# A seven-product MLP: four products of a pair accumulate in one PSUM bank that is read between them, two in a second bank

## The chip, the core and the metric

The kernel runs on one core of a Trainium2 chip. The metric is the device time of one execution in microseconds. Before the change the median of three runs is 2589.54 us (2586.69 to 2592.21).

The engines are called as the profile calls them: PE is TensorE's matrix multiplication and PEld its loading of weights, DVE is VectorE, ACT is ScalarE, POOL is GpSimd, and SP issues most of the DMAs. PSUM is the small memory into which matmuls write; a bank of it holds one result of 128 x 512 numbers here. ACT and DVE can read it. The kernel's tile framework puts in all the semaphores: an instruction that reads or writes a tile waits for the earlier ones on that tile. Each engine has one queue, whose order is fixed when the program is built.

## The reference

One decoder layer over 2048 tokens of width 1024 in f32: a mixer (retention and pooling heads), a cross-attention into 256 memory tokens, a gated MLP, each behind a row norm and with a residual, and a final norm. The change touches the MLP alone (`w_up` is 1024 x 5632, `w_down` 2816 x 1024):

```
def conv_glu_ffn(h, w_up, conv_w, conv_b, w_down):
    a = h @ w_up
    a1, a2 = a shifted by one and by two tokens
    c = conv_w[0] * a2 + conv_w[1] * a1 + conv_w[2] * a + conv_b
    gate, val = jnp.split(c, 2, axis=-1)
    return (jax.nn.silu(gate) * val) @ w_down
```

## The kernel before

**Passes.** Every f32 product is made of three matmuls on a high and a low half of each operand (`passes`, lines L226, L227 and L228: high by high, high by low, low by high). The high half is a rounded copy, the low half what the rounding left.

**Seven products.** Both halves of the MLP multiply in blocks of two by two with seven products in place of eight, in the manner of Strassen and Winograd. The weights' blocks are a11, a12, a21, a22 (rows: the two output tiles of a pair; columns: two halves of the contraction), and the right-hand side's are the two halves of the contraction by two halves of 512 tokens. Such a set of seven is a `Member`: `Up` (a gate column tile and its value column tile, 22 for each half of the tokens, 44 in all) or `Down` (two output tiles of 128 features and a third of the contraction: 4 pairs, 3 thirds, 2 halves of the tokens, 24 in all). A product is 4 x 3 matmuls of 128 x 128 by 128 x 512; in the first third of Down it is 3 x 3.

**The order.** `rounds` makes a `Round` for each half of the tokens for Up, then three for each half for Down. `run` goes through all products ("items") in order: round, group, product 0 to 6, member of the group. Up's first two and last two members form groups of two, whose products alternate; the 18 members between stand alone in each half of the tokens. Down's groups are all of two. After the matmuls of an item, `run` calls `fill` (prepares the operand of a later item: a sum of weight blocks on POOL, a high half on ACT, L990, a low half on DVE or, for one product, on POOL), takes a step of `pending` work, calls `evac` (takes the result out of PSUM), takes another step of `pending`, perhaps one of `later`, and moves the right-hand tiles on. Seven places (`prs`) hold prepared operands, so that they are made up to seven items ahead. The context is opened with `schedule_with_timeline_sim=True`: the order of an engine's queue can differ from the order of the text.

**Right-hand tiles.** A round's right-hand tiles (seven for each k, high and low, in G) are made by `combining` while the round before still runs: a load or two, a difference on POOL, a high half on ACT (L929), a low half on DVE or POOL. Scratch for it are the 512-wide places `TT`, eleven in all, which Up's evacuation and Down's residuals use too.

**Evacuation.** Each product has a PSUM bank of its own (`mmps`, five banks; three more, `aux`, serve other uses, among them the copies of `low`). Up's `evac` copies product 0 into the gate tile and into u (ACT, L1023), product 1 into q (ACT, L1028), and makes the other blocks from u, q and the banks with DVE (`tt`, L202). After product 4 the value's convolution (`conv`) joins `pending`, after product 6 the gate's: an activation (L1065), two multiply-adds on DVE (L211), Silu (L1077), a product, a store. Down's `evac` adds the products into a four-block accumulator Y, some into two blocks at once; `plain` and `rest` make the last differences and the residual, `out` the squares, the scaling and the store for the final norm.

## Time and profile before

| | before |
|---|---|
| median of the runs | 2589.54 us (2586.69 to 2592.21) |
| the profiled execution, first to last instruction | 2586.3 us; its record has no other time |
| instructions | 33008 |
| PE busy | 2469.2 us (95%) |
| PEld busy | 2047.5 us (79%) |
| DVE busy | 1983.9 us (77%) |
| ACT busy | 1229.4 us (48%) |
| POOL busy | 1094.9 us (42%) |
| mean granted TensorE clock | 0.981 |
| chain that ended last | PE 73%, DVE 11%, DMA 6%, POOL 4%, issue 4%, ACT 2% |

Busy time is the union of an engine's instructions. Matmuls overlap in the record, so that a matmul of 0.39 us can follow the one before after 0.23 us. A row of a group reads: line, engine, operation, output and inputs by tile, shape, count, then busy time, mean ns of one, idle time of the engine before them, and what ended it. "mm" and "aux" are PSUM banks; G, Q hold prepared halves, R raw weights, T scratch, Z the gate, value and Down's accumulators.

### The profile page before, as it was taken

How to read it: one execution, taken by the hardware profiler on the slowest of the kernel's cores; microseconds unless marked ns; L12 is line 12 of the kernel's file. 1: busy time of each engine (PE TensorE's matmuls, PEld its weight loads, DVE VectorE, ACT ScalarE, POOL GpSimd, SP SyncE). 2: the span in 40 equal slices, each digit the busy share in tenths (PEclk: the TensorE clock that was granted, in tenths of full speed). 3: DMA queues.
4: the chain of work that ended last, by engine and by line, in shares of the span. 5: the costliest groups of instructions: out<-in, count | busy, mean ns of one | idle time of the engine just before them, and what ended most of it. 6: DMA issues, size and time to landing. Idle time of an engine off the chain costs nothing.

```text
span 2586.3 us, 33008 instructions
## 1 busy us (share of the span) xinstructions
PE 2469.2 (95%) x11382; PEld 2047.5 (79%) x11382; DVE 1983.9 (77%) x2857; ACT 1229.4 (48%) x2222; POOL 1094.9 (42%) x816
## 2 busy tenths in 40 slices
PE   6899999999899999999899999989999989998996
PEld 5788887888688888888687888868888877786785
DVE  8846677657655675554899888898888898999996
ACT  4333423432221223423655656656655666666663
POOL 5221324007332122032544545874545586643661
PEclk8999999999899999999999999999999999998998
DMA  6133521202321101213343222432222356547751
GB/s 246 59 119 102 155 78 41 94 33 97 123 90 42 40 31 53 74 58 133 134 148 139 82 98 94 146 127 92 81 88 88 111 187 219 188 163 266 261 171 68
DMA packets 154648, 298.59 MB, mean 115 GB/s; under 512 B 15472, under 2 KB 37616, under 8 KB 154480
## 3 DMA queue, kind: packets, MB, share of 16 engines
q1 hardware_dynamic: 136304, 283.89, 32.2%
q10 hardware_dynamic: 18176, 12.59, 1.5%
q8 instruction: 90, 1.47, 0.2%
q14 instruction: 78, 0.64, 0.1%
HBM read 232.98 MB, written 63.44 MB: 115 GB/s over the span
## 4 chain that ended last, share of the span: by engine, by line
PE 73%; DVE 11%; DMA 6%; POOL 4%; issue 4%; ACT 2%; SPq 0%; DVEq 0%; POOLq 0%; ACTq 0%
PE mm L226 23%; PE mm L228 23%; PE mm L227 23%; DVE G L202 3%; DVE Z L202 3%; POOL T L202 2%; DMA T<-Gd 2%; DVE Q L202 2%; DVE T L202 1%; POOL R L202 1%; DMA T<-Hd 1%; DMA T<-Xd 1%; DVE Z L211 1%; DMA R<-w_v 1%; DMA T<-xT 1%
## 5 line engine op out<-in xcount | busy, mean ns | idle before, releaser
L226 PE MATMUL mm<-G,Q 128*128 128x512 f32 (+1 forms) x1944 | 755.3, 390 | 21.8 <-ACT Q L221 9.0
L228 PE MATMUL mm<-G,Q 128*128 128x512 f32 (+1 forms) x1944 | 753.8, 389 | 20.8 <-DVE Q L202 20.8
L227 PE MATMUL mm<-G,Q 128*128 128x512 f32 (+1 forms) x1944 | 752.8, 388 | 8.2 <-DVE G L202 6.9
L202 POOL TENSOR_TENSOR R<-R 128x512 f32<-128x512 f32 (+1 forms) x272 | 434.1, 1598 | 412.2 <-DMA R<-w_up 168.7
L226 PE MATMUL mm<-G 128*128 128x512 f32 (+1 forms) x1384 | 536.3, 388 | 23.4 <-DVE Z L202 11.4
L227 PE MATMUL mm<-G 128*128 128x512 f32 (+1 forms) x1384 | 535.5, 387 | 6.9 <-DVE G L202 6.3
L228 PE MATMUL mm<-G 128*128 128x512 f32 (+1 forms) x1384 | 533.9, 386 | 0.0
L226 PEld LDWEIGHTS mm<-G,Q 128*128 128x128 f32 x1944 | 372.6, 192 | 98.2 <-ACT Q L221 9.7
L228 PEld LDWEIGHTS mm<-G,Q 128*128 128x128 f32 x1944 | 372.2, 192 | 95.9 <-DVE Q L202 25.0
L227 PEld LDWEIGHTS mm<-G,Q 128*128 128x128 f32 x1944 | 372.6, 192 | 80.9 <-DVE G L202 9.8
L226 PEld LDWEIGHTS mm<-G 128*128 128x128 f32 x1384 | 261.9, 189 | 81.0 <-ACT Z L1023 9.7
L227 PEld LDWEIGHTS mm<-G 128*128 128x128 f32 x1384 | 262.0, 189 | 60.8 <-DVE G L202 8.7
L228 PEld LDWEIGHTS mm<-G 128*128 128x128 f32 x1384 | 261.5, 189 | 52.1
L211 DVE SCALAR_TENSOR_TENSOR Z<-Z,vecs 128x1024 f32<-128x1024 f32 x176 | 269.5, 1533 | 43.0 <-ACT Z L1065 41.4
L202 DVE TENSOR_TENSOR Q<-R,Q 128x512 fp32r<-128x512 f32 (+1 forms) x234 | 210.3, 900 | 113.3 <-ACT Q L221 108.0
L202 POOL TENSOR_TENSOR T<-T 128x512 f32<-128x512 f32 (+3 forms) x154 | 230.3, 1504 | 87.8 <-DMA T<-Gd 47.0
L202 DVE TENSOR_TENSOR Z<-Z,mm 128x512 f32<-128x512 f32 (+1 forms) x272 | 212.9, 786 | 35.3 <-PE mm L228 34.8
L221 ACT ACTIVATE Q<-R 128x512 fp32r<-128x512 f32 x150 | 94.1, 628 | 250.7 <-PE mm L227 185.1
L202 DVE TENSOR_TENSOR G<-T,G 128x512 fp32r<-128x512 f32 (+1 forms) x211 | 189.6, 909 | 29.0 <-ACT G L221 15.0
L990 ACT ACTIVATE G<-R 128x512 fp32r<-128x512 f32 (+1 forms) x272 | 164.0, 610 | 97.1 <-PE mm L227 64.8
L895 ACT ACTIVATE aux<-R 128x512 f32<-128x512 f32 (+1 forms) x272 | 153.4, 579 | 94.2 <-POOL R L202 60.2
L929 ACT ACTIVATE G<-T 128x512 fp32r<-128x512 f32 x210 | 129.1, 627 | 132.9 <-POOL T L202 90.2
(163 smaller groups left out, 3018.8 us busy)
## 6 DMA issues: line engine op xcount, KB each, us to landing
T<-Gd SPq DMA_DIRECT2D x198, 256.0 KB, 3.4
R<-w_up SPq DMA_DIRECT2D x176, 256.0 KB, 2.7
Gd<-Z SPq DMA_DIRECT2D x44, 512.0 KB, 2.6
T<-Hd SPq DMA_DIRECT2D x72, 256.0 KB, 3.0
R<-w_qkgu SPq DMA_DIRECT2D x32, 512.0 KB, 3.5
R<-w_dn SPq DMA_DIRECT2D x64, 256.0 KB, 3.5
T<-Xd SPq DMA_DIRECT2D x48, 256.0 KB, 3.6
R<-Md SPq DMA_DIRECT2D x16, 512.0 KB, 3.6
```

The source lines that it names most:

```text
L202: return eng.tensor_tensor(out=out, in0=a, in1=b, op=op)
L211: dve.scalar_tensor_tensor(out=out, in0=a, scalar=s, in1=b, op0=op0, op1=op1)
L221: act.activation(hi, src, AF.Copy)
L226: pe.matmul(ps, lh, rh, start=start, stop=False)
L227: pe.matmul(ps, lh, rl, start=False, stop=False)
L228: pe.matmul(ps, ll, rh, start=False, stop=stop)
L895: act.activation(t, x, AF.Copy)
L929: act.activation(hi, x, AF.Copy)
L990: act.activation(p2[:, 0, :w], x, AF.Copy)
```

## The change

The seven products come in another order and with other sums, so that the results add up inside PSUM. A member has three banks: A takes products 0, 2, 4 and 6, B takes 1 and 5, C (one of the `aux` banks) takes 3. A matmul into a bank that is in use goes on adding to what lies there; only products 0, 1 and 3 start a bank anew. Between the products A is read: after product 0 it holds one block or a part of one, after 2, 4 and 6 another. B is read after product 4 and again after 5.

- Up's `evac`: A is copied by ACT after 0, 2, 4 and 6 (gate, gate, value, value); DVE adds C to the gate after 3, B to the value after 4, B to the gate after 5. u and q are gone. The gate's convolution joins `pending` after 5, the value's after 6; the value tile is taken at 4.
- Down's `evac`: the same pattern, with ACT's copies only in the first third and DVE additions of one block each elsewhere. `plain` and `rest` are gone; the residual is four additions, and `out` runs for blocks 0, 3, 1, 2 after products 3, 4, 5, 6.
- Weights: a member needs its blocks a little earlier; the sums are one each for products 1, 2, 4 and 5. H is gone, and its two places join the raw weights' (ten in place of eight).
- Right-hand tiles: the differences chain through products 1, 2 and 6, and the partial one keeps its scratch place from 1 to 6 (from 1 to 3 before).

```diff
-    def passes(ps, lhs, rhs, start, stop):
+    def passes(ps, lhs, rhs, start, stop, more=False):
+
         (lh, ll), (rh, rl) = lhs, rhs
-        pe.matmul(ps, lh, rh, start=start, stop=False)
...
+        pe.matmul(ps, lh, rh, start=start, stop=False, skip_group_check=more)
...
     def combining(rd, i, j):
...
-        if i in (0, 5, 6):
-            r = load(k1 if i == 0 else k2, 1 if i == 5 else 0)
-        elif i in (1, 4):
-            r = load(k1, 1)
-            q = load(k2 if i == 1 else k1, 1 if i == 1 else 0)
-        else:
-            q = load(k1 if i == 2 else k2, 0)
-        yield
-        yield
-        if i in (2, 3):
-            r = rd.held[j]
+        r = load(*((k1, 0), (k1, 1), (k2, 1), (k2, 0), (k2, 1), (k2, 1), (k2, 0))[i])
+        if i in (1, 4):
+            q = load(k1, 0 if i == 1 else 1)
+        yield
+        yield
+        if i in (2, 6):
+            q = rd.held[j]
         x = r.f[:, :SUB]
         if q is not None:
-            a, b = (q, r) if i == 2 else (r, q)
-            tt(pool, x, a.f[:, :SUB], b.f[:, :SUB], ALU.subtract)
+            tt(pool, x, x, q.f[:, :SUB], ALU.subtract)
             q.free()
-            if i == 1:
+            if i in (1, 2):
                 rd.held[j] = r
...
         def add(self, i):
 
-            while len(self.raw) < (1, 2, 3, 3, 3, 4, 4)[i]:
+            while len(self.raw) < (1, 3, 3, 4, 4, 4, 4)[i]:
                 fetches.pop(0).fetch()
...
             if i == 1:
-                self.t = H.take()
-                x = self.t.f[:, :w]
-                tt(pool, x, *((a11, a21) if self.sign > 0 else (a21, a11)), ALU.subtract)
+                tt(pool, a21, a21, a22, ALU.add)
             elif i == 2:
-
-                tt(pool, a21, a21, a22, ALU.add)
                 tt(pool, a11, a21, a11, ALU.subtract)
-                x = a11
+            elif i == 4:
+                tt(pool, a21, a22, a11, ALU.subtract)
             elif i == 5:
-                tt(pool, a11, a12, a11, ALU.subtract)
-                x = a11
-            else:
-                x = {0: a11, 3: a22, 4: a21, 6: a12}[i]
-            return x, self.t
+                tt(pool, a12, a12, a11, ALU.subtract)
+            return (a11, a21, a11, a12, a21, a12, a22)[i]
...
+        def bank(self, i):
+
+            at = "ABACABA"[i]
+            if at not in self.banks:
+                self.banks[at] = aux() if at == "C" else mmps()
+            return self.banks[at]
...
         def evac(self, i, ps):          (Up)
...
-            if i == 2:
-                tt(dve, u, u, ps, ALU.add)
-            elif i == 3:
-                tt(dve, q, u, q, ALU.subtract)
-                tt(dve, val[0], q, ps, ALU.subtract)
-            elif i == 4:
-                tt(dve, gate[1], u, ps, ALU.add)
-                tt(dve, val[1], q, ps, ALU.add)
...
-                pending.extend(self.conv(1))
+            if i == 0:
+                act.activation(gate[0], ps, AF.Copy)
+            elif i == 2:
+                act.activation(gate[1], ps, AF.Copy)
+            elif i == 3:
+                tt(dve, gate[0], gate[0], ps, ALU.add)
+            elif i == 4:
+                act.activation(val[1], ps, AF.Copy)
+                tt(dve, val[1], val[1], self.banks["B"], ALU.add)
             elif i == 5:
                 tt(dve, gate[1], gate[1], ps, ALU.add)
-            else:
-                tt(dve, gate[0], gate[0], ps, ALU.add)
                 pending.extend(self.conv(0))
+            elif i == 6:
+                act.activation(val[0], ps, AF.Copy)
+                pending.extend(self.conv(1))
...
         def evac(self, i, ps):          (Down)
...
+            def take(q, ps):
+                if self.at == 0 and i in (0, 2, 4, 6) and ps is self.banks["A"]:
+                    act.activation(four[:, q], ps, AF.Copy)
+                else:
+                    tt(dve, four[:, q], four[:, q], ps, ALU.add)
+
+            if i != 1:
+                take((0, None, 1, 0, 3, 1, 2)[i], ps)
+            if i == 4:
+                take(3, self.banks["B"])
...
-                passes(ps, w, (right(i, j, 0), right(i, j, 1)), j == 0, j == rd.n - 1)
+                passes(ps, w, (right(i, j, 0), right(i, j, 1)), j == 0 and i in (0, 1, 3), j == rd.n - 1, i in (2, 4, 5, 6))
...
-    raws = Places([(R, j * SUB) for j in range(8)], SUB)
-    H = Places([(R, 4 * T + i * SUB) for i in range(2)], SUB)
+    raws = Places([(R, j * SUB) for j in range(10)], SUB)
```

More of the change, by code (lines that the diff above doesn't have):

```diff
@@ L950, in __init__ @@
             self.loads, self.n = loads, halves
-            self.sign, self.how = 1, ("", "copy", "copy", "", "copy", "copy", "")
-            self.raw = {}
+            self.how = ("", "copy", "copy", "", "copy", "copy", "")
+            self.raw, self.banks = {}, {}
         def fetch(self):
@@ L1009, in __init__ @@
             self.c = {}
-        def bank(self, i):
-            return mmps()
         def place(self):
@@ L1087, in five @@
                 after(2, store)
-            return [one, two, three] + ([] if g else [four, five])
+            return [one, two, three, five if g else four]
     class Down(Member):
@@ L1128, in evac @@
                 self.took = 0
-                for q in range(3):
-                    later.append(lambda q=q: self.residual(q, ALU.subtract if q else ALU.add))
+                for q in range(4):
+                    later.append(lambda q=q: self.residual(q))
             if self.at < 2:
```

80 lines of the change are left out of this document (22 added, 58 removed).

## The prediction

> **What bounds the kernel now.** I read the page first, for the engines and the slices; then the table of windows over the MLP (which begins near 1240 us); then TensorE's waits from there on; then the groups of instructions with their shapes; and last the order of time at single places. From the page:
>
> ```profile
> span 2586.3 us, 33008 instructions
> PE 2469.2 (95%) x11382; PEld 2047.5 (79%) x11382; DVE 1983.9 (77%) x2857; ACT 1229.4 (48%) x2222; POOL 1094.9 (42%) x816
> PE   6899999999899999999899999989999989998996
> DVE  8846677657655675554899888898888898999996
> ```
>
> TensorE is the bound over the whole span, and in the second half of the slices VectorE stands at eight and nine tenths beside it. Four windows tell the stages of the MLP apart (columns: length; busy time and count of PE, PEld, DVE, ACT, POOL; granted clock; DMA):
>
> ```profile
> 1650.00:1700.00 50.00, 42.01 (x177) 33.08 (x176) 46.25 (x43) 32.02 (x53) 48.03 (x35) 0.99 0.46 156
> 1850.00:1900.00 50.00, 50.00 (x222) 41.42 (x221) 41.46 (x47) 31.19 (x48) 25.31 (x20) 1.00 0.22 80
> 2100.00:2150.00 50.00, 41.60 (x174) 33.34 (x173) 44.15 (x57) 34.68 (x69) 32.21 (x23) 0.93 0.57 189
> 2400.00:2450.00 50.00, 44.26 (x177) 34.06 (x176) 48.74 (x61) 32.19 (x59) 33.93 (x22) 0.93 0.71 240
> ```
>
> In the run of single Up pairs (1850 to 1900) TensorE is full: there is nothing to win there, only to lose. At the change from the first half of the tokens to the second (1650), from Up to Down (2100) and inside Down (2400), TensorE loses 6 to 8 us in 50 and VectorE is at 44 to 49 of 50. What TensorE waited for from 1260 us to the end (total, times, longest):
>
> ```profile
> PE mm L226 <- DVE Z L202: 13.8, 8, 5.6
> PE mm L227 <- DVE G L202: 10.7, 7, 4.1
> PE aux L1219 <- DVE Q L202: 9.0, 2, 5.8
> PE mm L226 <- ACT G L929: 3.0, 3, 1.6
> PE aux L298 <- DVE T L202: 2.3, 1, 2.3
> PE mm L227 <- POOL G L202: 1.9, 2, 1.4
> ```
>
> "DVE Z" is a read of a PSUM bank that VectorE finishes late, so that a later product finds no bank; "DVE G" is the low half of a right-hand tile made late; "DVE Q" is the row-norm's chain, once between the halves (5.8) and once at the end. VectorE ends 13.8 + 10.7 + 5.8 = 30.3 us in the body, the rest of "Q" and "T" lies in the tail.
>
> **The change, part by part.** First the unit of time, the matmul, and what happens where a product ends:
>
> ```profile
> 1878.10 0.39 PE L226 MATMUL mm<-G 128*128 128x512 f32 x1
> 1879.92 0.39 PE L228 MATMUL mm<-G 128*128 128x512 f32 x1
> 1880.14 0.39 PE L226 MATMUL mm<-G 128*128 128x512 f32 x1
> 1880.17 0.63 ACT L990 ACTIVATE G<-R 128x512 fp32r<-128x512 f32 x1 [1.09 <-PE mm L227]
> 1880.34 1.28 DVE L202 TENSOR_TENSOR Z<-T,mm 128x512 f32<-128x512 f32 x2 [0.67 <-PE mm L228]
> 1882.86 0.39 PE L226 MATMUL mm<-G 128*128 128x512 f32 x1
> ```
>
> From 1878.10 to 1882.86 lie 21 matmuls: 0.2267 us each, so 2.72 us for a product of twelve (2.04 for nine), 19.04 for a pair's seven. The matmul of 1879.92 is the last of an Up pair's product 4, and it ends at 1880.31.
>
> *VectorE's and ScalarE's work on the results.* The rows (whole span):
>
> ```profile
> L202 DVE TENSOR_TENSOR Z<-Z,mm 128x512 f32<-128x512 f32 x216 | 145.6, 677 | 31.7 <-PE mm L228 31.3 <-ACT Z L1119 0.2
> L202 DVE TENSOR_TENSOR Z<-T,mm 128x512 f32<-128x512 f32 x132 | 86.2, 681 | 17.8 <-PE mm L228 14.7
> L202 DVE TENSOR_TENSOR T<-T,mm 128x512 f32<-128x512 f32 x76 | 51.5, 680 | 23.3 <-PE mm L228 22.8
> L202 DVE TENSOR_TENSOR T<-T 128x512 f32<-128x512 f32 x170 | 153.8, 911 | 10.0 <-ACT T L335 6.7 <-ACT T L1148 1.5 <-DMA T<-Yd 0.3
> L202 DVE TENSOR_TENSOR Z<-Z,mm 128x1024 f32<-128x1024 f32 x56 | 67.6, 1208 | 3.6 <-PE mm L228 3.5
> L202 DVE TENSOR_TENSOR Z<-Z 128x512 f32<-128x512 f32 x16 | 13.8, 864 | 0.1
> L1028 ACT ACTIVATE T<-mm 128x512 f32<-128x512 f32 x44 | 25.8, 587 | 0.0
> L1065 ACT ACTIVATE Z<-Z,vecs 128x1024 f32<-128x1024 f32 x88 | 109.4, 1243 | 143.7 <-DVE Z L202 143.7
> ```
>
> An Up pair has seven VectorE operations now (u plus bank 0.68, u minus q 0.91, three of 0.68 into Z, two of 0.68 for products 5 and 6: 4.99 us) and three copies on ScalarE. After the change it has three additions (2.03 us) and four copies. So VectorE loses 2.96 us and ScalarE gains 0.59 per pair of 19.04: over 44 pairs -130 and +26 us. In Down the first sixth of a column has 4 x 0.68 + 1.21 = 3.93 on VectorE now and three additions, 2.04, after; the second and third have three double additions and four single ones, 6.34, against seven single ones, 4.76. With 8 and 16 pairs that is 15 + 25 us less; the 16 subtractions Z<-Z (0.86) go as well, 14 us; the residual's additions stay four to a pair (three and one apart now). VectorE sheds some 184 us in all. Almost none of it is on the path: under the single pairs TensorE is full anyway. It counts where VectorE is behind.
>
> *Where VectorE is behind.* Of the 30.3 us the bank waits (13.8) are hit twice, by fewer operations and by half of the reads moving to ScalarE, which is at 32 to 35 of 50; the late low halves (10.7) only by fewer operations, and a pair's two convolutions now queue up one product apart at its end, so that some of VectorE's work moves later, into the change of stages. Bounds: nothing, if other work fills the place, and 30.3, if all go. I take half, 15. Long waits cost again behind themselves:
>
> ```profile
> 1698.07 0.50 PE L227 MATMUL mm<-G,Q 128*128 128x512 f32 x1 [4.08 <-DVE G L202]
> 1698.74 0.63 PE L226 MATMUL mm<-G,Q 128*128 128x512 f32 x1
> 1699.17 0.63 PE L227 MATMUL mm<-G,Q 128*128 128x512 f32 x1
> 1701.30 0.63 PE L226 MATMUL mm<-G,Q 128*128 128x512 f32 x1
> ```
>
> After a wait of 4.08 us the matmuls come 0.43 us apart, some nine of them, 9 x 0.20 = 1.8 us lost. Four such places would be 7 us; half of them gone is 3.5. [...]
>
> *The tail.*
>
> ```profile
> 2559.63 0.39 PE L227 MATMUL mm<-G 128*128 128x512 f32 x1
> 2559.81 2.08 DVE L202 TENSOR_TENSOR T<-T 128x512 f32<-128x512 f32 x3
> 2561.81 0.68 DVE L202 TENSOR_TENSOR Z<-Z,mm 128x512 f32<-128x512 f32 x1
> ```
>
> The last matmul starts one slot later, at 2559.86, and ends at 2560.25; its result is added at 2561.81, behind three additions of squares. After the change one output comes out at each of products 3 to 6 and the two subtractions are gone, so that the queue should be empty: 1.5 us won, between 0 and 1.6.
>
> *The new waits.* Bank A is read after products 0, 2, 4, 6 and written again by the next of them. Between lies one other product in a single pair (2.72 us) and three in a group of two. The reader is ScalarE: one preparation that becomes ready at the same moment, 0.63, then the copy, 0.59: 1.2 us, within 2.72. With a convolution's activation of 1.24 ahead as well it is 2.5, still within; only a second one would cost, 1.0 us. I take nothing.
>
> Bank B is the sharp one. After product 4 the kernel copies A into the value half and then adds B to it on VectorE; only then may product 5 write B, and in a single pair product 5 comes next. The chain from the rows: last matmul ends 1880.31, ScalarE is at its preparation until 1880.80, the copy takes it to 1881.39, the addition of 0.68 to 1882.07. Product 5 would have begun at 1880.14. That is 1.9 us in each of the 36 single pairs (18 in each half): 67 us, if TensorE has nothing else in that place. Behind the waiting matmul stand product 6 and the next pair, and behind those the preparations on ScalarE that wait for their buffers. Does the queue hold something else there? Its order need not be that of the text:
>
> ```profile
> 2404.73 0.39 PE L226 MATMUL mm<-G,Q 128*128 128x512 f32 x1
> 2404.95 0.39 PE L226 MATMUL mm<-G 128*128 128x512 f32 x1
> 2405.18 0.39 PE L227 MATMUL mm<-G,Q 128*128 128x512 f32 x1
> 2405.64 0.39 PE L227 MATMUL mm<-G 128*128 128x512 f32 x1
> ```
>
> The text issues L226, L227, L228 in turn for one product. Here two products are woven matmul by matmul, without a gap: where an operand was expected late, the queue was built with other work in front. Seven operand buffers let the next pair's product 0 be ready three products ahead. So I expect some eight matmuls of it, and then some of product 6, in front of product 5. What remains is the error of that planned order against the chip. Bounds 0 and 1.9 us a pair; nearest is the woven row, without a gap; I take one matmul slot, 0.23, a pair: 8 us. [...] In groups of two a whole product (2.04 or 2.72) lies between, above 1.9: nothing, at most the same slot in 32 pairs, 7 us.
>
> *Edits with one answer.* The matmuls are the same in number and length. GpSimd makes four sums to a weight pair and four to a right-hand tile as before, the loads are as many, and two more places for raw weights let them start earlier; none of it is on the path in the full windows: nothing. Product 3 takes one of three "aux" banks for 2.72 us; the copies that share them are four in 19 us: nothing. A right-hand tile's partial difference now keeps a scratch place from its second product to its last, four of eleven places, but Up gives up two to a pair: nothing in Up, see the rivals for Down.
>
> **Sum.** -15 - 3.5 - 1.5 + 8 = -12 us on the profiled execution's 2586.3, 2574.3. That execution lies 3.2 under the median of 2589.54; on the median it is 2577.
>
> **Rivals.**
> *Slower: bank B's wait lies open.* Place: before product 5 of the 36 single pairs. In full, 67 - 20 gained: 2589.5 + 47 = 2637; half open, 2603. It decides from 20 / 36 = 0.56 us a pair. For it: TensorE has no idle time there that could absorb anything, and the order of the queue cannot answer to a late engine. Against it: the woven rows, and a VectorE that drops from 41.46 of 50 by 2.96 in 19.04, to about 34, in that stage.
> *No change: the relief doesn't reach TensorE.* The late right-hand tiles are bound by GpSimd (48.03 of 50 in the first row of windows) and by the convolutions that moved later; only the tail's 1.5 and a quarter of the waits, 7.5, come, against 8 lost: 2588.5, within 0.2% (5 us, about what a measurement here can tell from no change).
> *Slower in Down: scratch places.* Four held places delay the right-hand tiles: the 10.7 + 3.0 + 1.9 us of waits on G double, +16, and the other gains halve to 5: 2601 with no loss elsewhere.
>
> **How the numbers follow.** Forecast 0.53 (its own range 2562 to 2583: half of its waits and the slot moved by half and double), bank B open 0.20, no change 0.20, scratch 0.07. The low end is the forecast with nearly all of VectorE's waits gone and no slot lost (-30.3 - 7 - 1.5 = -39, 2551): 2553 leaves 0.04 below. The high end, 2608, takes in the scratch case and half-open banks and leaves some 0.12 above. Faster by over 0.2%: 0.53 and a little of the second rival, 0.55; within: 0.18; slower: 0.27.
>
> **What would show it.** Right: VectorE's busy time near 1800 us and ScalarE's near 1255; windows of single pairs still at about 222 matmuls in 50 us; matmuls of the next pair between products 4 and 5; less waiting for "DVE Z" in the windows of 1650, 2100 and 2400. Wrong: a wait of TensorE for VectorE's read once in every 19 us (bank B), or for ScalarE's copy (bank A); full single pairs with the same 30 us lost at the changes of stage (no change); more waits for G in Down (scratch).

## The result, and the profile after

The changed kernel takes 2614.26 us (median; 2611.70 to 2614.86) against 2589.53 of the kernel before on the same chip: a ratio of 1.0097, 95% interval 1.0083 to 1.0111, some 25 us slower. The forecast was 2577 and the range ended at 2608: the sign was wrong. The profiled execution took 2614.86 with this span and these busy times:

```profile
span 2613.1 us, 32538 instructions
PE 2480.7 (95%) x11382; PEld 2052.6 (79%) x11382; DVE 1813.1 (69%) x2649; ACT 1249.6 (48%) x2266; POOL 1080.3 (41%) x816
```

VectorE sheds 170.8 us (184 were said) and ScalarE gains 20.2 (26 were said). The work went where the change put it; the time did not follow. The four windows of the prediction, now of the changed kernel (columns as there):

```profile
1650.00:1700.00 50.00, 36.31 (x156) 29.37 (x155) 45.12 (x43) 34.60 (x59) 46.21 (x33) 0.90 0.59 194
1850.00:1900.00 50.00, 50.00 (x222) 41.42 (x221) 33.62 (x39) 30.38 (x49) 27.00 (x19) 1.00 0.22 71
2100.00:2150.00 50.00, 42.31 (x169) 33.80 (x168) 40.03 (x43) 31.23 (x58) 33.82 (x22) 0.86 0.44 148
2400.00:2450.00 50.00, 47.23 (x205) 37.58 (x203) 42.42 (x53) 34.42 (x64) 37.56 (x26) 1.00 0.85 282
```

The single Up pairs (1850) are as full as before, 222 matmuls, with VectorE down from 41.46 to 33.62 of 50. The change of halves (1650) makes 156 matmuls where it made 177. (The last window lies at another point of its round than before, and is not to be compared by itself.) What TensorE waited for from 1260 us to the end, total, times, longest:

```profile
PE mm L227 <- ACT Z L1019: 15.5, 3, 11.1
PE mm L227 <- ACT Z L1098: 13.9, 3, 6.2
PE mm L229 <- DVE Q L202: 10.8, 6, 4.4
PE mm L227 <- ACT Q L979: 7.9, 6, 2.4
PE aux L1186 <- DVE Q L202: 4.3, 2, 3.3
PE mm L227 <- DVE Z L202: 4.0, 6, 1.2
PE mm L228 <- DVE G L202: 3.0, 4, 1.5
PE aux L227 <- DVE G L202: 2.8, 2, 2.4
```

The line tells which operand is late: L227 is the first pass and reads both high halves and a bank, L228 takes the low half of the tile, L229 the low half of the weights (L226, L227, L228 before). So "ACT Z" is the copy of the standing bank A (L1019 product 0 in Up, L1098 the same in Down); L229, and L227 on ScalarE's L979, are weights; and "aux L227" on VectorE is the third bank, C, which still holds a copy that VectorE has not read: the first pass needs no operand of VectorE's. Before, "DVE Z" led with 13.8, tiles (L227 there) followed, and weights had one row of 0.6.

Both lists begin at 1260, and the MLP some 20 us earlier. Between 1225 and 1260 TensorE waited 9.6 us before the change and 2.9 after it. Most of it before was for ScalarE's copies of product 0; counted from 1225 on, the kernel before has the row

```profile
PE mm L226 <- ACT Z L1023: 8.4, 3, 6.7
```

of which 0.7 lies behind 1260. This matters for the sums below.

The longest waits of the changed kernel, in order of time on ScalarE and then on TensorE (start, length, in brackets the idle time before and what ended it; other rows are left out):

```profile
1686.61 0.63 ACT L925 ACTIVATE G<-T 128x512 fp32r<-128x512 f32 x1 [0.99 <-POOL T L202]
1688.81 0.63 ACT L925 ACTIVATE G<-T 128x512 fp32r<-128x512 f32 x1 [1.57 <-POOL T L202]
1689.34 0.61 ACT L979 ACTIVATE Q<-R 128x512 fp32r<-128x512 f32 x1
1691.61 0.63 ACT L925 ACTIVATE G<-T 128x512 fp32r<-128x512 f32 x1 [1.65 <-POOL T L202]
1695.48 0.63 ACT L979 ACTIVATE G<-R 128x512 fp32r<-128x512 f32 x1 [3.24 <-POOL R L202]
1696.54 1.04 ACT L1058 ACTIVATE Z<-Z 128x1024 f32<-128x1024 f32 x1
1697.48 0.58 ACT L1019 ACTIVATE Z<-mm 128x512 f32<-128x512 f32 x1
```

```profile
1686.64 0.39 PE L229 MATMUL mm<-G 128*128 128x512 f32 x1
1698.11 0.80 PE L227 MATMUL mm<-G 128*128 128x512 f32 x1 [11.08 <-ACT Z L1019]
```

The copy of 0.58 us that frees bank A stands behind three tile halves and, at 1695.48, a weight half, each of which waits for an operation of GpSimd's, and behind a Silu (L1058). And in Down, where a weight half is late (other rows left out again):

```profile
2446.31 0.63 ACT L925 ACTIVATE G<-T 128x512 fp32r<-128x512 f32 x1 [0.55 <-POOL T L202]
2447.99 0.63 ACT L925 ACTIVATE G<-T 128x512 fp32r<-128x512 f32 x1 [1.04 <-POOL T L202]
2448.53 0.61 ACT L979 ACTIVATE Q<-R 128x512 fp32r<-128x512 f32 x1
2449.19 0.50 PE L227 MATMUL mm<-G,Q 128*128 128x512 f32 x1 [2.06 <-ACT Q L979]
2452.39 0.61 ACT L979 ACTIVATE Q<-R 128x512 fp32r<-128x512 f32 x1
2453.59 0.68 DVE L202 TENSOR_TENSOR Q<-R,Q 128x512 fp32r<-128x512 f32 x1
2454.32 0.79 PE L229 MATMUL mm<-G,Q 128*128 128x512 f32 x1 [4.39 <-DVE Q L202]
```

The weight's high half is made at 2448.53, right behind a tile half that GpSimd released at 2447.99, and TensorE takes it at once.

### The profile page after: what moved, and what is told of

Same layout as the page of the kernel before. It is cut to its first block, busy times and chain, and to the rows that moved or that the text cites. A ratio compares the mean times of both kernels' runs of the same rounds, so it can differ in the third digit from the quotient of the medians.

```text
span 2613.1 us, 32538 instructions
## 1 busy us (share of the span) xinstructions
PE 2480.7 (95%) x11382; PEld 2052.6 (79%) x11382; DVE 1813.1 (69%) x2649; ACT 1249.6 (48%) x2266; POOL 1080.3 (41%) x816
## 4 chain that ended last, share of the span: by engine, by line
PE 73%; DVE 11%; DMA 5%; POOL 5%; issue 3%; ACT 3%; SPq 0%; DVEq 0%; POOLq 0%; ACTq 0%
PE mm L229 21%; PE mm L227 21%; PE mm L228 21%; DVE G L202 3%; POOL T L202 3%; DVE Z L202 2%; DMA T<-Gd 2%; DVE Q L202 2%; PE aux L227 2%; PE aux L228 2%; PE aux L229 2%; POOL R L202 1%; DVE T L202 1%; DVE T L211 1%; DMA T<-Hd 1%
## 5 line engine op out<-in xcount | busy, mean ns | idle before, releaser
L227 PE MATMUL mm<-G,Q 128*128 128x512 f32 (+1 forms) x1884 | 734.0, 391 | 33.3 <-ACT Q L979 9.5
L229 PE MATMUL mm<-G,Q 128*128 128x512 f32 (+1 forms) x1884 | 730.7, 390 | 32.9 <-DVE Q L202 32.9
L228 PE MATMUL mm<-G,Q 128*128 128x512 f32 (+1 forms) x1884 | 731.2, 388 | 4.1 <-DVE G L202 4.0
L202 POOL TENSOR_TENSOR R<-R 128x512 f32<-128x512 f32 (+1 forms) x272 | 428.1, 1580 | 321.3 <-DVE G L202 108.0
L227 PE MATMUL mm<-G 128*128 128x512 f32 (+1 forms) x1180 | 456.1, 389 | 25.9 <-ACT Z L1019 13.7
L228 PE MATMUL mm<-G 128*128 128x512 f32 (+1 forms) x1180 | 455.8, 387 | 2.1 <-DVE G L202 2.1
L229 PE MATMUL mm<-G 128*128 128x512 f32 (+1 forms) x1180 | 451.4, 386 | 0.5 <-DVE G L202 0.5
L229 PEld LDWEIGHTS mm<-G,Q 128*128 128x128 f32 x1884 | 361.7, 192 | 108.5 <-DVE Q L202 39.9
L227 PEld LDWEIGHTS mm<-G,Q 128*128 128x128 f32 x1884 | 362.3, 192 | 107.4 <-ACT Q L979 12.7
L228 PEld LDWEIGHTS mm<-G,Q 128*128 128x128 f32 x1884 | 362.2, 192 | 74.7 <-DVE G L202 7.4
L211 DVE SCALAR_TENSOR_TENSOR Z<-Z,vecs 128x1024 f32<-128x1024 f32 x176 | 259.8, 1488 | 61.4 <-ACT Z L1046 60.5
L227 PEld LDWEIGHTS mm<-G 128*128 128x128 f32 x1180 | 223.7, 190 | 76.5 <-ACT Z L1019 14.5
L228 PEld LDWEIGHTS mm<-G 128*128 128x128 f32 x1180 | 224.0, 190 | 46.6 <-DVE G L202 3.4
L229 PEld LDWEIGHTS mm<-G 128*128 128x128 f32 x1180 | 223.6, 190 | 45.4 <-DVE G L202 0.9
L979 ACT ACTIVATE G<-R 128x512 fp32r<-128x512 f32 (+1 forms) x272 | 165.5, 610 | 145.9 <-PE mm L228 119.8
L202 DVE TENSOR_TENSOR G<-T,G 128x512 fp32r<-128x512 f32 (+1 forms) x211 | 198.8, 952 | 47.3 <-ACT G L925 31.4
L202 DVE TENSOR_TENSOR Z<-Z,mm 128x512 f32<-128x512 f32 x232 | 156.4, 678 | 104.9 <-PE mm L229 104.8
L202 DVE TENSOR_TENSOR G<-aux,G 128x512 fp32r<-128x512 f32 (+1 forms) x239 | 159.7, 671 | 62.8 <-ACT aux L896 31.2
```

The lines of the kernel that those rows point to most:

```text
L202: return eng.tensor_tensor(out=out, in0=a, in1=b, op=op)
L211: dve.scalar_tensor_tensor(out=out, in0=a, scalar=s, in1=b, op0=op0, op1=op1)
L227: pe.matmul(ps, lh, rh, start=start, stop=False, skip_group_check=more)
L228: pe.matmul(ps, lh, rl, start=False, stop=False, skip_group_check=more)
L229: pe.matmul(ps, ll, rh, start=False, stop=stop, skip_group_check=more)
L979: act.activation(p2[:, 0, :w], x, AF.Copy)
```

## The experiments

Times are medians, ratios are to the kernel before in the same batch. Two measures are used beside them. *Loss*: the spacing of consecutive matmul starts less 0.2267 us, summed over a stretch; "changes" are 1225 to 1420, 1620 to 1780 and 2060 to 2180 us together, "Down" is 2180 to 32 us before the end. *Waits* of TensorE from 1260 on, as the profile lists them, sorted by line and releaser as just told: banks A and B (reads into Z or T), bank C (a first pass that waits for VectorE), tiles, weights; "all" has the norm's too. S stands for "the reads of the standing bank A are late", P for "scratch places", C for "coupled sums of weights, GpSimd late", A for "bank C shares the aux banks".

**How much is the change's own.** In four runs one neutral number of the plan moved, the spread of the tiles' due times:

```diff
-                    at += 22 / (7 * rd.n)
+                    at += 21 / (7 * rd.n)      (23 in the two "wide" ones)
```

The changed kernel with 21: 

> The changed kernel with one number of the due times of right-hand tiles changed (21 in place of 22 items for a round's tiles), which none of the theories minds: it tells how much the time moves with the order that is planned. All theories: 2614 within 4 us. If it moves by 8 us or more, differences of that size between the other runs tell nothing.

The kernel before with 21: 

> The kernel before with one neutral number of its plan changed (the due times of the right-hand tiles spread over 21 products' share instead of 22), as was done with the changed kernel (-6 us). If that 6 us is noise of the order that any edit shuffles: within 6 us of 2589.5 on either side. If the due times themselves are too late in both kernels: about -6 us again.

The kernel before with 23: 

> The kernel before with the other neutral step of the same number (23 for 22; with 21 it became 0.5% slower). If the plan before stands on a lucky order and any edit costs it about 10 us: 2596 to 2604, and some 10 of the change's 25 us are not the change's own. If 21 was merely too tight: 2586 to 2592.

The changed kernel with 23: 

> The changed kernel with 23 for 22 in the due times of the tiles, the third point of its neutral neighbours (22: 2614.3, 21: 2608.2; before: 22: 2589.5, 21: 2600.8, 23: 2596.5). If order luck is of about 6 us on either side: 2606 to 2618. The difference of the two triples is then the change's own cost.

| kernel | us | ratio [95%] | loss: changes | loss: Down | banks A, B | bank C | tiles | weights | all |
|---|---|---|---|---|---|---|---|---|---|
| before | 2589.5 | 1 | 36.2 | 32.0 | 17.5 | 0 | 15.6 | 0.6 | 45.0 |
| before, 21 | 2600.8 | 1.0050 [1.0035, 1.0066] | 39.4 | 39.9 | 20.1 | 0 | 16.4 | 3.8 | 55.4 |
| before, 23 | 2596.5 | 1.0026 [1.0016, 1.0037] | 42.9 | 34.7 | 18.6 | 0 | 21.5 | 0 | 46.0 |
| after | 2614.3 | 1.0097 [1.0083, 1.0111] | 48.3 | 45.5 | 33.6 | 2.8 | 3.8 | 19.2 | 67.5 |
| after, 21 | 2608.2 | 1.0075 [1.0056, 1.0094] | 45.5 | 41.0 | 22.7 | 11.7 | 1.6 | 21.9 | 63.4 |
| after, 23 | 2614.1 | 1.0098 [1.0082, 1.0114] | 49.0 | 47.7 | 22.7 | 12.6 | 0 | 22.4 | 66.5 |
| Up changed only | 2599.5 | 1.0039 [1.0024, 1.0054] | 48.0 | 29.6 | 28.2 | 5.2 | 6.8 | 5.3 | 56.7 |
| Down changed only | 2611.7 | 1.0084 [1.0065, 1.0102] | 40.1 | 46.6 | 13.1 | 7.4 | 10.4 | 15.8 | 54.3 |

Both neutral steps made the kernel before slower, by 7 and 13 us in their own batches, and the changed one 6 us faster or not at all. So the plan before stood at a good order, by luck or because 22 had been chosen for it; the record doesn't tell. The mean of the three is 2595.6 before and 2612.2 after: by these few points 16.6 us are the change's own, and some 8 of the 25 belong to the order. The means of all waits from 1260 on are 48.8 and 65.8. The rows show which; the changed kernel with 21, then with 23:

```profile
PE mm L227 <- ACT Q L979: 11.5, 6, 4.0
PE aux L227 <- DVE Q L202: 9.3, 3, 7.4
PE mm L229 <- DVE Q L202: 7.1, 6, 2.2
```

```profile
PE mm L229 <- DVE Q L202: 11.3, 7, 3.0
PE mm L227 <- ACT Q L979: 10.7, 6, 2.8
PE aux L227 <- DVE Q L202: 10.2, 3, 8.8
```

Late weights and the third bank, of which the kernel before has next to nothing in any of its three runs; its largest are these, with 21 and with 23:

```profile
PE mm L226 <- DVE Z L202: 17.3, 12, 3.0
PE mm L227 <- POOL G L202: 8.4, 1, 8.4
```

```profile
PE mm L226 <- DVE Z L202: 17.1, 11, 5.9
PE mm L227 <- DVE G L202: 16.9, 8, 5.5
```

So after the change TensorE waits 12 to 22 us less for tiles, and 18 to 22 more for weights and 3 to 13 more for bank C. Waits for A and B changed their reader, from VectorE to ScalarE. From 1260 on they are 3 to 4 us larger in the neighbours and 16 in the kernel itself. Counted from 1225 (25.2, 26.3 and 25.0 us before), they are 2 to 4 us smaller in the neighbours and 8 larger in the kernel itself, where Down's copies (L1098) take 13.9 us against 6.4 and 4.2; the long wait near 1698 is in all three (11.1, 8.0 and 9.5).

The classes name what came last at a place, and others can be late behind it: near 2126 the changed kernel waits 4.7 us for the copy of bank A, its neighbours 7.4 and 8.8 for bank C. What a class gains or loses is therefore not a cause by itself.

**One part alone.** Up as changed and Down as before, and the other way round; two classes side by side:

```diff
-            ups = [Up(b, f) for f in range(NF)]
+            ups = [Up(b, f) for f in range(NF)]          (UpOld in the second kernel)
-                ms = [Down(b, j, at, k0, n) for j in range(KT // 2)]
+                ms = [DownOld(b, j, at, k0, n) for j in range(KT // 2)]      (Down in the second)
```

Both keep the places of the kernel before, eight for raw weights and the two of H.

Up alone: 

> Up with its right-hand tiles, weights and banks as changed, Down with all of these as before. By the loss counted by stage (5 at Up's start, 5 at the change of halves, 1 at the change to Down, 17 in Down) Up alone should stand at 2600. Theory P, which bites in Down: 2595. Theory S: the reads out of bank A in Up keep their 15.5 us, those of Down's first third go: 2598. If Up alone is faster than 2589.5, the loss is Down's alone.

Down alone: 

> The other half alone: Up as before, Down with its right-hand tiles, weights and banks as changed (eight raw places and two for the separate sum, as before). By the count of stages Down loses 13.5 us of the 27 and Up's stages 12: 2602. Theory P (the held scratch places make Down's loads late) expects Down's stage as in the whole change, 43 to 48 us lost against 32: 2601 to 2606. Theory S expects the copies of Down's first third (13.9 us) to be seen again. If the halves' losses don't add (this one at 2590), they need each other at the change to Down.

Each half moves the loss of its own stages (table): with the changed Up the changes of stage lose 45.5 to 49.0 us against 36.2 to 42.9, with the changed Down that stage loses 41.0 to 47.7 against 29.6 to 39.9. But both stretches together lose 77.6 us with Up alone, which lies among the 68.2, 79.3 and 77.6 of the kernel before and its neighbours, as its time does; with Down alone they lose 86.7. So, by one run of each, a cost beyond the order is seen for Down, and for Up it isn't shown. Down alone was expected at 2602; of the 24 us between its profiled execution and that of the kernel before, some 5 lie ahead of 1225. The banks' waits come with Up (28.2), the weights' with Down (15.8).

**The standing bank (S).** All of its copies on VectorE instead of ScalarE:

```diff
-                act.activation(gate[0], ps, AF.Copy)
+                dve.tensor_copy(gate[0], ps)             (and the four others)
```

> Theory S (the standing read): bank A's copy waits in ScalarE's in-order queue behind halves of right-hand tiles that are late, and TensorE needs the bank back; it ended 15.5 us (L1019) and 13.9 us (L1098) of TensorE's waits after the change. With all copies out of bank A on VectorE, half to all of the 29 us goes: 2585 to 2600 against 2614. Theory C (coupled sums: GpSimd's in-place weight sums wait for VectorE's low halves, and operands come late) and theory P (scratch places: the held partial difference makes right-hand loads late): no gain, 2614, or up to 10 us more, since VectorE has 4 x 44 + 32 operations more.

2629.81 us, 1.0162 [1.0145, 1.0179]. Banks A and B fall to 18.2 us of waiting (3.5 of it one wait behind a step of the norm), and others take the place, above all bank C with 22.0 (from 1260 on):

```profile
PE aux L227 <- DVE Q L202: 14.7, 5, 9.9
PE aux L227 <- DVE G L202: 7.3, 2, 3.9
```

The copies issued right after their product's matmuls, ahead of the weights' high half; once in the changed kernel and once with the changed Up alone:

```diff
+            early = not norm and i in (0, 2, 4, 6) and not (isinstance(m, Down) and not Y)
+            if early:
+                m.evac(i, ps)
             if not norm:
                 fill()
...
-            m.evac(i, ps)
+            if not early:
+                m.evac(i, ps)
```

> The changed kernel with one thing moved: ScalarE's copies of bank A (products 0, 2, 4, 6) are issued straight after the product's matmuls, ahead of the high half of the weights, the SiLU and the convolution that stood before them in ScalarE's queue. In all six variants of the changed kernel looked at, TensorE stands 8 to 12 us near 1690 for the copy of product 0 (L1019), and each time ScalarE stood at another thing (a sum of GpSimd's, a convolution step of VectorE's). Theory S: these waits (ACT Z 15.5 at the change of halves, 13.9 in Down) fall to under 8 together; the loss at the change of halves falls from 16.8 to about 9 us, time 2596 to 2604. Rival: the tiles are late there in any order, and the wait for the copy only hides a wait for G behind it: ACT Z falls, waits for G and Q take its place, 2608 to 2618.

> The Up pairs as changed and Down as before (2599.5 so far), with the copies of bank A first. Theory S: the copies' waits at the change of halves (ACT Z 9.2 us) and at the change to Down (8.6 us) fall to about 5 in all: 2584 to 2592, the first variant that could beat the kernel before. Rival (tiles late in any order): 2596 to 2603.

2613.88 us, 1.0098 [1.0081, 1.0114], and 2600.93, 1.0044 [1.0029, 1.0059]: nothing in either. In the first the copy near 1697 still stands where it did, behind the same tile halves and the same weight half: the order of ScalarE's queue came out the same there (why isn't shown), and so did TensorE's waits:

```profile
PE mm L227 <- ACT Z L1019: 15.4, 3, 11.1
PE mm L227 <- ACT Z L1098: 11.7, 3, 4.7
```

So this run did not take the wait away and does not settle what it would be worth; the run with VectorE took half of it away and gained nothing, but gave VectorE 208 copies more. The kernel before with one bank less to rotate through:

```diff
-    mmp = ctx.enter_context(tc.tile_pool(name="mmp", bufs=5, space=bass.MemoryType.PSUM))
+    mmp = ctx.enter_context(tc.tile_pool(name="mmp", bufs=4, space=bass.MemoryType.PSUM))
```

> The kernel before with four banks for the products in place of five: a result must be read within three products, as bank A's in a group of two after the change. Theory S (what was lost is the time that a result may wait): waits for reads of banks at the changes of stage grow, and the MLP loses a good part of 12 to 27 us: 2600 to 2615; some of it may come in the stages before the MLP, which use the same banks. Theories C and P: within 5 us of 2589.5 in the MLP.

2620.98 us, 1.0119 [1.0098, 1.0141]; some 10 us of its loss lie ahead of 1225, the rest in the MLP, with the wait for banks at

```profile
PE mm L226 <- DVE Z L202: 24.2, 20, 3.9
```

against 13.8 (17.3 and 17.1 in the neighbours): fewer banks to choose from do cost at these stages.

**Scratch places (P).** Two places more for two places of raw weights less:

```diff
-    raws = Places([(R, j * SUB) for j in range(10)], SUB)
+    raws = Places([(R, j * SUB) for j in range(8)], SUB)
+    for j in (8, 9):
+        TT.freed.append(len(TT.one))
+        TT.one.append(Arena(R, j * SUB, 1, SUB))
```

> Two of the ten places for raw weights become scratch places (thirteen in place of eleven). Theory P: the loads of right-hand tiles start earlier, GpSimd's wait for them in Down (91 us, 43 before the change) and the loss in Down (17 of the 25 us) shrink by half: 2600 to 2606. Theories S and C: 2612 to 2618.

2609.64 us, 1.0083 [1.0066, 1.0100]: no better than a neutral step, and short of the half that theory P expected. Yet Down's loss fell from 45.5 to 34.8 us, and GpSimd's wait for the tiles' loads (2110 to 2600 us) with it; the kernel before, the changed kernel, and this run:

```profile
POOL T L202 <- DMA T<-Gd: 43.2, 18, 9.1
```

```profile
POOL T L202 <- DMA T<-Gd: 91.3, 37, 8.0
```

```profile
POOL T L202 <- DMA T<-Gd: 53.7, 20, 7.5
```

Of the 10.7 us that Down won, the changes of stage lost 2.9 again (51.2 us against 48.3), with two raw places less, and bank C's waits stand at 17.5. The profiled execution, the fastest of the four, is 7.5 us shorter than that of the changed kernel, the median 4.6. Weights are as late with eight raw places (18.5 us) as with ten. The other way to free places is not to hold the difference from product 2 to 6:

```diff
-        if i in (2, 6):
+        if i == 2:
             q = rd.held[j]
         x = r.f[:, :SUB]
+        if i == 6:
+            tt(pool, x, x, right(2, j, 0).bitcast(F32), ALU.subtract)
+            tt(dve, x, x, right(2, j, 1).bitcast(F32), ALU.subtract)
...
```

> The changed kernel, but the right-hand difference of product 2 is not held in a scratch place until product 6: product 6 takes it back from the two halves of product 2's operand that lie in G (one subtraction more on GpSimd and one on VectorE for each tile of product 6, results equal up to the last bits). Theory P: up to four of eleven scratch places come free, GpSimd's wait for T<-Gd loads in Down falls from 91 us to about 50, Down's loss from 45 to 30 or 35, time 2598 to 2604. Theory C / GpSimd as the bound: four more GpSimd operations of 1.7 us at each change make the losses larger, 2614 to 2624. Theory S: no change, 2608 to 2620.

2635.29 us, 1.0182 [1.0165, 1.0199], the slowest of all, with 54.7 lost in Down and 58.6 at the changes. Theory P said the opposite. One row of ScalarE's waits (1225 to 2600 us) is new:

```profile
ACT G L929 <- DVE T L202: 38.4, 17, 3.9
```

L929 is the tile's high half in this kernel. A chain one operation longer at product 6 makes ScalarE stand 38 us for VectorE's part of it, and TensorE's waits grow from 67.5 to 74.9 us. The run does not isolate the places; that the longer chain is what costs is likely, and not shown by itself.

**GpSimd (C).** The weights' sums on VectorE, and, apart from that, no low halves on GpSimd:

```diff
-                tt(pool, a21, a21, a22, ALU.add)
+                tt(dve, a21, a21, a22, ALU.add)          (and the three other sums)
```

```diff
-        low(x, hi, lo, "pool" if rd.shared and (i * rd.n + j) % 3 == 2 else "copy" if i in (1, 2) else "")
+        low(x, hi, lo, "copy" if i in (1, 2) else "")
...
-            self.b, self.f, self.how = b, f, ("", "copy", "copy", "", "copy", "copy", "pool")
+            self.b, self.f, self.how = b, f, ("", "copy", "copy", "", "copy", "copy", "")
```

> The changed kernel with the four sums of a member's weights on VectorE instead of GpSimd. Theory C (the change couples the sums in place, and GpSimd, busy 61.2 of 65 us at 1650:1715 and standing in order at late right-hand loads in Down, makes the weights late): some 11 sums of 1.65 us leave GpSimd at the change of halves, so the loss there falls from 16.8 to about 8 us; in Down the waits for Q (9.6 + 4.9 us) fall to about 4; time 2590 to 2598. Theory P (scratch places held from product 1 to 6): Down goes on losing about 45 us, time 2604 to 2614. Theory S (ScalarE's reads of bank A stand in its queue behind tiles that GpSimd owes): ScalarE's waits at the change of halves (13.7 us) shrink with GpSimd's load, those in Down (6.2 us) stay; time about 2605.

> The changed kernel with no low half on GpSimd; VectorE, which the change relieved, makes them all. If GpSimd is the bound at the change of halves (61.2 of 65 us busy, 11 low halves of 18.4 us among it), the loss there falls from 16.8 to about 8 us and the rest stays: about 2605. Theory P alone: no change in Down (45 us) and, since places come free no sooner, 2608 to 2614. Theory S: VectorE's room is used, ScalarE's copies of bank A wait less for GpSimd's sums: 2603 to 2608.

2604.48 us, 1.0072 [1.0056, 1.0088], and 2605.81, 1.0070 [1.0055, 1.0085]: the best with both parts changed, but by less than the neutral steps move a kernel. At the change of halves GpSimd was at 61.2 of 65 us; with the sums on VectorE:

```profile
1650.00:1715.00 65.00, 51.51 (x209) 41.07 (x209) 61.98 (x64) 40.30 (x69) 48.23 (x32) 0.89 0.56 191
```

GpSimd has room, VectorE is at 61.98, and TensorE makes 209 matmuls instead of 214. GpSimd alone is not the bound there. Nor are its sums all that makes weights late: 16.0 us of weights' waits are left of 19.2.

**The low halves' copies (A, and ScalarE's load).** All of the weights' low halves through an aux bank, and none:

```diff
-            self.how = ("", "copy", "copy", "", "copy", "copy", "")
+            self.how = ("copy", "copy", "copy", "copy", "copy", "copy", "")      (none: seven times "")
```

> Products 0 and 3 make their low half from a PSUM copy of the raw weights, as products 1, 2, 4, 5 do, so that GpSimd's in-place sum for products 2 and 5 waits for a ScalarE copy and not for VectorE. Theory C: the waits of TensorE for weights' halves (DVE Q 10.8, ACT Q 7.9) go: 2595 to 2600. Theory S: ScalarE's queue gets two copies more a pair, 0.58 us each, and the bank's read comes later: 2615 to 2625. Theory P: 2614.

> The changed kernel with every low half of the weights made straight from the raw place, without ScalarE's copy into an aux bank. ScalarE loses four copies a pair (2.3 us in 19), the aux banks are bank C's but for the tiles' copies; VectorE's low halves get longer (0.92 in place of 0.68) and GpSimd's sums wait for them. Theory S and theory A (bank C stands behind copies for VectorE in the aux banks, seen in two of the variants as waits of TensorE for an aux bank): 2595 to 2605. Theory C: the weights come later still, 2620 to 2630. Theory P: 2614.

2608.39 us, 1.0072 [1.0057, 1.0087], and 2624.36, 1.0135 [1.0116, 1.0154]. With copies everywhere TensorE waits 30.3 us for bank C, nearly all of it

```profile
PE aux L227 <- DVE Q L202: 29.8, 5, 9.2
```

and with none there is no such row at all: theory A's mechanism is shown, bank C waits for copies that share its three banks. They are the weights' copies: the right-hand tiles still copy through these banks in the run with none. But other waits move the other way: with copies everywhere weights and banks A and B fall to 6.0 and 13.6 us, without them the weights rise to 40.9, where VectorE makes every low half straight from the raw places (73% busy on the mean, and yet late).

**SP's queue.** In Down the weights' loads issued by GpSimd:

```diff
-            sp.dma_start(r.f[:, :w], self.loads[g][:, h * w : (h + 1) * w])
+            (pool if isinstance(self, Down) else sp).dma_start(r.f[:, :w], self.loads[g][:, h * w : (h + 1) * w])
```

> The changed kernel with Down's loads of weights (R<-w_dn, 86 of them) issued by GpSimd instead of SP. In the changed kernel SP stands 32.8 us at loads of weights whose place waits for a sum of GpSimd's, and the loads of right-hand tiles stand behind them in the same queue; GpSimd then waits 91 us for T<-Gd. If this queue is what makes Down's tiles late: the wait for T<-Gd falls to about 60, Down's loss from 45.5 to 34 to 38, time 2602 to 2607. Rival (GpSimd's own order and the scratch places set the pace, or the issue itself costs GpSimd time): Down stays at 43 to 52, time 2608 to 2622.

2625.33 us, 1.0134 [1.0112, 1.0156]. GpSimd's wait for the tiles' loads did fall, but the issue costs GpSimd time, and SP stands for scratch places instead (2110 to 2600 us; waits of GpSimd, of SP, and the group of issues with busy time, mean ns and idle time):

```profile
POOL T L202 <- DMA T<-Gd: 65.3, 33, 5.9
```

```profile
SPq L907 <- DVE G L202: 88.2, 51, 14.7
```

```profile
L956 POOL DMA_DIRECT2D R<-w_dn x86 | 47.1, 548 | 40.7 <-DVE G L202 23.0 <-ACT G L979 5.6 <-ACT Q L979 4.7
```

So the rival held, and beyond its range: taking the weights' loads out of SP's queue did not help. As they then stand in GpSimd's queue, the run does not tell what a free queue would be worth.

**Together.** The copies first, two scratch places more, and the sums on VectorE (the three diffs above):

> The copies first (as in the run beside it), two scratch places more for two raw places less, and the weights' sums on VectorE, together: each alone was worth 5 to 10 us or is expected to be. If they take off different waits (S at the changes, P and C in Down): losses of about 9 at the change of halves and 33 in Down, 2586 to 2594, level with the kernel before. If all of them only shuffle one order around a bound that the tiles set: 2600 to 2608, no better than the best of them alone.

2610.48 us, 1.0082 [1.0065, 1.0098]: the partial gains do not add; Down's loss is 44.6 again. No version beat the kernel before.

## Why the prediction was wrong

*What held.* VectorE's and ScalarE's busy times and the full single pairs came as said, and so did the step that was thought the sharpest. Bank B's chain stays covered: a copy of A (L1025) at 1875.66, the addition of B on VectorE at

```profile
1877.78 0.67 DVE L202 TENSOR_TENSOR Z<-Z,mm 128x512 f32<-128x512 f32 x1
```

and TensorE goes from the first to the last of these 24 matmuls without a gap meanwhile:

```profile
1874.89 0.39 PE L227 MATMUL mm<-G,Q 128*128 128x512 f32 x1
...
1880.11 0.39 PE L229 MATMUL mm<-G,Q 128*128 128x512 f32 x1
```

Of the +8 taken for it nothing shows, and the rival of 67 us (36 x 1.9 is 68) fell. The waits that the term "half of VectorE's 30.3 us", -15, was to shorten did shrink: DVE Z fell from 13.8 to 4.0 (3.4 and 4.2 in the neighbours) and the tiles' waits from 15.6 to 3.8. How much of that is VectorE's relief isn't shown, since half of the reads went to ScalarE and a tile that comes late behind a late weight shows no wait.

*Bank A: "I take nothing".* This failed. The step counted ScalarE's own work before the copy (a preparation and an activation, 2.5 us against 2.72) and did not ask what that work waits for. At a change of stage the instructions ahead of the copy stand for GpSimd's tiles and sums, and the copy with them: 29.4 us for ACT Z (L1019 and L1098), a single wait of 11.1 among them. The kernel before has such waits too, 9.6 us from 1225 on, all but 1.9 of them ahead of the 1260 where the prediction began to count. On the means of the three, from 1225 on, waits for ScalarE's reads of banks grew from 8.2 to 22.5 us and those for VectorE's reads into Z fell from 16.1 to 3.9; the reads into T, 1.2, are gone. Net, A and B cost 0.8 us more: what the change took off VectorE's reads came back as ScalarE's.

*"Aux": nothing.* This failed too. The step counted four copies in 19 us of a single pair. At the changes and in Down VectorE reads such copies late, and bank C waits for it: 2.8 us in the changed kernel, 11.7 and 12.6 in its neighbours, 9.0 on the mean.

*Edits with one answer: "none of it is on the path: nothing".* This failed, and is the largest part: 19.7 us more of waits for weights, on the means. The step looked at the full windows, where it is true, and counted operations, which are as many. What moved is their place in the round: a tile's subtraction is made at products 1, 2, 4, 6 now. Numbering the 210 tile halves of L925 (L929 before) in the plan's order, ScalarE's waits in Down for GpSimd at products 4 and 6 are 21.5 and 12.0 us, before 5.4 and 0; at products 1 to 3 they fell from 41.1 to 20.2. Numbering the 476 high halves of weights (L979) in the same way, the four in Down that TensorE waits for are all product 0 of a group's first member: an operand without any sum, which in the rows of 2446 to 2449 stands behind tile halves. These four are 4.9 of the 19.2 us; 10.8 are low halves of weights that VectorE makes late, among them the 4.39 us at 2454. At that place an addition Z<-Z,T of VectorE's took 1.75 us at 2448.43, while four tile operations of GpSimd's ran, and 0.68 at 2454.19, so that what runs beside VectorE is one more suspect that no run took away. That the order of the sums is the cause is read from these traces; no run put the subtractions back to products 1 to 4 with all else as changed, so it is argued and not shown. The run with the longer chain at product 6 is slower by 21 us, but its weights' waits are no larger (17.9), so it doesn't settle this either. Of the other suspects, the loads' queue, GpSimd's share and the scratch places, each alone was tried, and none recovers much more than a neutral step does.

*Scratch places: "nothing in Up", and a rival at 2601 with 0.07.* The mark of that rival, GpSimd's wait for T<-Gd, more than doubled (43.2 to 91.3). The run with two more places puts their weight at some 10 us in Down; but the waits on G, which it expected to double, fell.

*The tail, -1.5.* The prediction took the matmul at 2559.86 for the last; the view goes on to

```profile
2561.22 0.39 PE L228 MATMUL mm<-G 128*128 128x512 f32 x1
```

which ends at 2561.61, so that the addition at 2561.81 was 0.2 us behind it and not 1.5. After the change it is 0.04 behind (2588.09 and 2588.13): that little was there to win.

*The slow clock after long waits, -3.5.* It went the other way. The spacing of matmuls over 0.2267 us without a wait of their own adds up to 13.5 us from 1225 on before and 22.4 after (with 21 and 23: 17.3 and 22.9 before, 18.9 and 25.7 after), 4.4 more on the means; behind the wait of 11.08 us the matmuls come 0.43 us apart, with a granted clock of 0.50 from 1698 to 1703.

*The reference point.* The forecast took the plan before as an ordinary one. Two neutral steps made it 0.26 and 0.50% slower, and an edit that moves the order can give that up. This alone reaches past the 5 us that were called "no change".

In sum, on the means of the three and from 1260 on: tiles -16.0, norm -3.6, weights +19.7, bank C +9.0, banks A and B +7.6, other +0.3: +17.0 us of waiting. That this is near the 16.6 us of time is chance. From 1225 to 1260 the change saved 5.6 us (8.5 before, 2.8 after), most of it waits for the copies of product 0, so that the MLP as a whole waits some 11 us more; the rest of the loss (75.0 and 92.3 us at the changes and in Down together) is slower spacing around the waits. The reads and tiles that were expected to cost less did, and the steps that were expected to cost nothing cost more than that. So the step that failed most is "none of it is on the path: nothing", with 19.7 us of waits for weights in place of nothing. Why the weights come late stays open as said, and so does whether a bank of its own for C, with five left for A and B, would bring the changed kernel level: no run tried it.

## What to carry to other kernels

The bank that stood between products tied TensorE here to what its reader's earlier instructions waited for: 11.08 us for a copy of 0.58 us, whose matmuls had ended by 1687.03, while ScalarE stood 3.24 us for a sum of GpSimd's ahead of it. So ask not how long the reader is busy before the read, but what the instructions ahead of it wait for, at the worst stage. Adding no operation did not make a step free: with as many sums as before, TensorE waited 19.7 us more for weights on the means. The suspect, argued above and not shown, is a step moved within its round and what then stands behind it; look at the first operand of the next group. And before a gain of half a per cent is forecast for a plan written out by hand, move a neutral number of it by one step in both kernels: here that alone was worth up to 0.5%.

## What the runs showed that was not expected

A change of one number in the due times, with the same work, moved the kernel before by 0.26 and 0.50% (7 and 13 us) and the changed one by up to 6 us. With Down's weights issued by GpSimd, a DMA kept it busy 548 ns each (86 of them, 47.1 us). With 171 us of VectorE's work gone the whole was no faster: TensorE is 95% busy in both, and from 1650 to 1700, where it lost most of the four windows (36.31 of 50 us busy), VectorE stood at 45.12, GpSimd at 46.21 and ScalarE at 34.60: no queue was full over the whole of it, though VectorE was from 1682 to 1698 (16.00 of 16).
